# Square sums behind the FFN's first product copies, residuals from PSUM, and samples' states one by one, in a hybrid decoder layer

## The chip, the core and the metric

The kernel runs on one core of a Trainium2 chip. A core has TensorE (PE), which multiplies matrices into PSUM; VectorE (DVE), ScalarE (ACT) and GpSimd (POOL), which work on elements; and SyncE (SP), from which this kernel issues its DMAs. Each engine takes its own instructions strictly in the order in which the program lists them, and waits on semaphores for the others. The metric is the device time of one execution in microseconds, the median of some runs.

## The reference

One layer of a hybrid decoder, for a prompt of 16 + 1024 rows and 8 samples of 8 rows, each row 1024 wide. What matters here:

```
proj = rmsnorm(h) @ w_in                  # short convolution and SSD inputs
ya   = group_rmsnorm(gate_b * conv(gate_c * hv))
y, s = ssd_chunked(...)                   # chunks of 128; a state per head, sample and prompt
yb   = group_rmsnorm((y + D * xs) * silu(z))
mix  = concat(ya, yb) @ w_out
h    = h + rmsnorm(mix, norm_mix_post)
fn   = rmsnorm(h, norm_ffn_pre)
f    = (silu(fn @ w_gate) * (fn @ w_up)) @ w_down
h    = h + rmsnorm(f, norm_ffn_post)
```

Each rmsnorm multiplies a row by the inverse root of its mean square and by a weight. The outputs are the new rows and the new states.

## The kernel before

The kernel is written with pools of named tiles. A planner, which runs when the program is built, puts the instructions of each engine in order by priorities and by its own estimate of their times, places the tiles, and adds the semaphores. `high_priority(offset=n)` moves the instructions of a block ahead by n places in that order. So the order on the chip is fixed, but not the one in which the code is written, and an edit in one place can move instructions elsewhere. Products in float32 accuracy are made of three matmuls each, on a rounded high part and a low rest of both factors; each such split is a copy on ACT and a subtraction on DVE.

There are 10 tiles of rows: 0 is the 16 meta rows, 1 to 8 are the prompt, 9 is the samples. The work goes through these stages.

- *Projection and chunks.* The product with `w_in` (line 220) fills PE throughout. In between lie the SSD chunks 1 to 8 (`ssd_chunk`, with high priority HP1), and behind each chunk some of the 8 pieces of the samples' states (`sample_state(u)`, priority HP2). The table SAMP says which piece follows which chunk: one behind chunks 1, 2, 5 and 6, two behind 3 and 4. A piece loads states (tile s0, line 747), transposes them on PE into the PSUM tile s0p (line 750), splits them (s0t, lines 752 to 755), adds the update from PE's tile s1p (lines 760 to 766), stores them through SP (line 769), and multiplies by the samples' C (line 773). Two pieces in a row share the masked tiles bm1 and bm2, which the even one builds (line 740). s0p and s1p come from a pool of two PSUM tiles of two banks each, which the chunks use too. The chunk loads its decay matrix M with a DMA (line 548); DVE and ACT work on it at lines 553 to 558.

- *Output projection.* GROUPS are three groups of three tiles, (1, 2, 3), (4, 9, 5) and (6, 7, 8). For each group the 12 blocks of `w_out` are loaded and split (lines 995 to 1000) and multiplied with the three tiles' mix (line 1009), each tile into two accumulators of 512 columns. `bank` gives out accumulators in turn: positions 0 and 1 of each six are single banks, the other four are halves of two-bank tiles. Each group starts at position 2, so its first and second tile get one two-bank tile each, and the third gets two single banks. In the last group's last block the order of tiles is 8, 6, 7. After a group, `h_tile` copies each tile's two halves from PSUM into the SBUF tile h, one half on ACT (line 887), one on DVE (line 888).

- *Residual and second norm.* `residual(i, h)` takes the square sum of h on ACT (line 147, instructions named ms), the root on POOL (line 141, mr), scales h on DVE (line 899), adds the input rows (line 900) and stores h through SP (line 901). `fn_tile(i, h)` takes a second square sum (hs), root (hr), and scales into hn (line 916). PE transposes hn into the PSUM tile fT (line 928), from which ACT copies the plain transposed rows xr (line 933) and splits follow (lines 936 and 937). All square sums write their squares into one junk tile. For the first two groups this runs inside the next group's matmuls; for the last group it stands where the FFN begins, with priority HP4.

- *FFN.* The products with `w_gate` and `w_up` are made from seven products of half matrices (a Strassen-like scheme) in 11 steps. For the first three steps one of the seven, and its extension, is made ahead by `first(q)`: for x = g and u, PE multiplies the first half into the accumulator (called xg or xu, line 1050), ACT copies it out as p1g or p1u (line 1079); then PE adds the second half onto the same accumulator, ACT takes Silu of one (line 1083) and DVE the product (line 1084). The operands of `first` come from tiles 1 to 4 and 9, so the first one doesn't need the last group. It stands in the code between the last group's residuals and its `fn_tile`s. Then DVE forms sums of the xr's (T1 to T4, B22, lines 1194 to 1204 and 1190 to 1191) and of the weights (line 1091 and on; their splits, named s2g and so on, at lines 1042 and 1043), and `rest(q)` makes the other products (yg, yu, zg, zu). In two places the first column of a tile is written from p1u ahead of the tile itself (line 1189): that holds the tile's instructions behind p1u.

- *Down projection* (line 1393) and the last norm.

Of the kernel before, what the change touches and what calls it, by code (L numbers as in the profile page):

```python
# [8 lines left out]
F32 = mybir.dt.float32  # L9
# [7 lines left out]
P = 128  # L17
# [19 lines left out]
NACC = 2  # L37
YB = 1
SKIP = NMETA - 4
SAMP = {1: (0,), 2: (1,), 3: (2, 3), 4: (4, 5), 5: (6,), 6: (7,)}  # L40
LATE = (9,)
WIDE = True
SORD = "c0 c1 v0 v1 b0 c2 b1 v2 c3 v3 b2 b3"
# [13 lines left out]
def hymba_kernel(ctx, tc, x_prompt, x_sample, state_sconv, state_ssm_conv, state_ssm, meta_tokens,  # L57
# [79 lines left out]
    def rstd_of(ss, w, d, name):  # L137
        v = tp.tile([P, 1], F32, tag="rv", name=name, bufs=4)
        V.tensor_scalar(out=v[:w], in0=ss[:w], scalar1=1.0 / d, scalar2=EPS, op0=ALU.mult, op1=ALU.add)
        r = tp.tile([P, 1], F32, tag="rr", name=name + "r", bufs=4)  # L140
        G.tensor_tensor(out=r[:w], in0=v[:w], in1=mhalf[:w], op=ALU.pow)
        return r

    def square_sum(pool, src, w, name):
        junk = pool.tile([P, DM], BF16, tag="junk", name=name + "j", bufs=1)
        ss = tp.tile([P, 1], F32, tag="ss", name=name, bufs=6)
        S.activation(junk[:w, :], src, AF.Square, accum_out=ss[:w])
        return ss
# [49 lines left out]
    def bank(name):  # L198
        q = turn[0] % 6
        turn[0] += 1  # L200
        if q < 2:
            return ps.tile([P, 512], F32, tag="acc", name=name, bufs=NACC)
        if q % 2 == 0:
            turn[1] = big(name)
        return turn[1][:, (q % 2) * 512:(q % 2) * 512 + 512]
# [676 lines left out]
    def h_tile(i, pts):  # L882

        t0, w = TT[i]
        h = ph.tile([P, DM], F32, tag="h", name=f"h{i}", bufs=3)
        if w == P:
            S.activation(h[:, 0:512], pts[0], AF.Copy)
            V.tensor_copy(h[:, 512:], pts[1])
        else:
            for c in range(2):  # L890
                merge(h[:w, c * 512:(c + 1) * 512], pts[c], w, f"hm{i}{c}", ph)
        return h

    def residual(i, h):
        t0, w = TT[i]
        r = rstd_of(square_sum(ph, h[:w, :], w, f"ms{i}"), w, DM, f"mr{i}")
        xt = ph.tile([P, DM], F32, tag="tok", name=f"xt2{i}", bufs=3)
        SY.dma_start(xt[:w, :], x_rows(i))
        V.scalar_tensor_tensor(out=h[:w], in0=h[:w], scalar=r[:w], in1=post_bc[:w], op0=ALU.mult, op1=ALU.mult)
        V.tensor_tensor(out=h[:w], in0=h[:w], in1=xt[:w], op=ALU.add)  # L900
        SY.dma_start(d_h[i][:, :], h[:w])

# [6 lines left out]

    psf = []  # L910

    def fn_tile(i, h):
        t0, w = TT[i]
        xt = ph.tile([P, DM], F32, tag="tok", name=f"hn{i}", bufs=3)
        r = rstd_of(square_sum(ph, h[:w, :], w, f"hs{i}"), w, DM, f"hr{i}")
        V.scalar_tensor_tensor(out=xt[:w], in0=h[:w], scalar=r[:w], in1=ffn_bc[:w], op0=ALU.mult, op1=ALU.mult)
        late = i in GROUPS[-1]
        if late:
            both = psf[0].tile([P, 2, 512], F32, tag="pr", name=f"fT{i}", bufs=4)
        for q in range(2):  # L920
            if late:
                pt = both[:, q, :]
            else:
                pt = ps.tile([P, 512], F32, tag="small", name=f"fT{i}{q}", bufs=NSM)[:, :]
            pt = pt.rearrange("p (k t) -> p k t", k=4)
            for k in range(4):
                kk = 4 * q + k
                PE.transpose(pt[:, k, :w], xt[:w, kk * P:(kk + 1) * P], ident[:w, :w])
            for n, cs, ts in pieces(i):
                if q == 1 and i == GROUPS[-1][1]:  # L930
                    V.tensor_copy(xr[q][n][:, :, cs], pt[:, :, ts])
                else:
                    S.activation(xr[q][n][:, :, cs], pt[:, :, ts], AF.Copy)
                if n == 0:
                    bh, bl = (b[:, :, cs] for b in B1[q])
                    S.activation(bh, pt[:, :, ts], AF.Copy)
                    V.tensor_tensor(out=bl, in0=pt[:, :, ts], in1=bh.bitcast(F32), op=ALU.subtract)
# [49 lines left out]
    load_mix("b", GROUPS[0])  # L987
    for gi, tiles in enumerate(GROUPS):
        turn[0] = 2
        accs = {i: [bank(f"o{i}{c}") for c in range(2)] for i in tiles}  # L990
        for n, k in enumerate([4, 5, 6, 7, 8, 9, 10, 11, 0, 1, 2, 3]):
            nv = vec[:, 72 + k:73 + k]
            with tc.high_priority(offset=HPW):
                raw = wp.tile([P, DM], F32, tag="raw", name=f"wo{k}", bufs=3)
                SY.dma_start(raw, w_out[k * P:(k + 1) * P, :])
                hi = wp.tile([P, DM], F32R, tag="whi", name=f"woh{k}", bufs=2)
                lo = wp.tile([P, DM], F32R, tag="wlo", name=f"wol{k}", bufs=2)
                S.activation(hi, raw, AF.Copy, scale=nv)  # L998
                V.scalar_tensor_tensor(out=lo, in0=raw, scalar=nv, in1=hi[:, :].bitcast(F32), op0=ALU.mult,  # L999
                                       op1=ALU.subtract)  # L1000
            if n == 11 and gi + 1 == len(GROUPS):
                tiles = tiles[2:] + tiles[:2]
            for i in tiles:
                mh, ml = mix["b" if k >= 4 else "a", i]
                kb = k - 4 if k >= 4 else k
                steps = [(mh, hi), (mh, lo)] + ([(ml, hi)] if ml is not None else [])
                for q, (l, r_) in enumerate(steps):
                    for c in range(2):
                        PE.matmul(accs[i][c], l[:, kb, :], r_[:, c * 512:(c + 1) * 512],  # L1009
                                  start=n == 0 and q == 0, stop=n == 11 and q == len(steps) - 1)  # L1010
            if n == 1:
                load_mix("a", tiles)
            if n in (2, 6) and gi == 0:
                for q in LATE if n == 2 else FIN[9]:
                    finish(q)
            if n == 9 and gi + 1 == len(GROUPS):
                for x in "gu":
                    early_weights(x, 0)
            if n == 5 and gi + 1 < len(GROUPS):
                load_mix("b", GROUPS[gi + 1])  # L1020
            if n in RES and len(pend) > RES.index(n):
                residual(*pend[RES.index(n)])
            if n in FNS and len(pend) > FNS.index(n):
                fn_tile(*pend[FNS.index(n)])
        if gi + 1 == len(GROUPS):
            with tc.high_priority(offset=HPW):
                for x in "gu":
                    early_weights(x, 1)
        pend = [(i, h_tile(i, accs[i])) for i in tiles]

# [131 lines left out]
            residual(*args)  # L1164
    first(0)
    with tc.high_priority(offset=HP4):
        for args in pend:
            fn_tile(*args)
    first(1)
    phx.__exit__(None, None, None)  # L1170
    pmx.__exit__(None, None, None)
# [288 lines left out]
```

## Time and profile before

| | us |
|---|---|
| median of 3 runs | 1406.01 (1403.69 to 1406.12) |
| profiled execution | 1402.11 |
| its span, first to last instruction | 1400.4 |
| PE busy | 1369.7 |
| DVE busy | 973.9 |
| ACT busy | 586.2 |

A row of the timeline gives start and duration in us, engine, source line, operation, the tile written and the tiles read (out<-in), the shape and the number of instructions merged; in brackets the idle time of the engine just before it and the instruction that ended it. A row of the waits gives engine, line and tile that waited, the instruction that it waited for, the total in us, the number of waits and the longest. A row of the windows gives a stretch, its length, the busy time of PE, of PE's weight loads, of DVE, ACT and POOL with the number of their instructions, then TensorE's granted clock as a share of full speed, the DMA engines' share and GB/s. A row of one source line gives engine, operation and count, the shortest, median and longest duration in ns, and the first and last start. A busy PE is not PE at its peak, since its matmuls are pipelined and their ends are modelled.

### The profile page before, as it was taken

Reading aid. Unit: us, or ns where it says so; the run is one execution under the profiler, and the core shown is the slowest. Engines: PE = TensorE matmul, PEld = TensorE weight load, DVE = VectorE, ACT = ScalarE, POOL = GpSimd, SP = SyncE. Lnnn points to the kernel's source line nnn. Section 1 sums busy time; section 2 is a strip of 40 time slices with the busy share of each in tenths; the row PEclk is TensorE's granted clock in tenths of the full one; section 3 lists DMA queues with packets and bytes.
Section 4 is the critical chain, followed back from the end, with each engine's and each line's share of the span. In section 5 each row is a group of like instructions: output and inputs, shape, how many; then the busy total and the mean of one; then the engine's idle time right before and its main releaser. Section 6 shows DMA issues by size and latency. Waiting matters only on the chain.

```text
span 1400.4 us, 22011 instructions
## 1 busy us (share of the span) xinstructions
PE 1369.7 (98%) x8841; PEld 1230.6 (88%) x8841; DVE 973.9 (70%) x1334; ACT 586.2 (42%) x947; POOL 51.8 (4%) x106
## 2 busy tenths in 40 slices
PE   7999999999999999999899999999999999999997
PEld 5889998878888988887799999999999998888886
DVE  6654457868888988767689877666767666455565
ACT  6465345434354354656553232222332334344431
POOL 1000000000000200011100000000000000000001
PEclk9999999999999999999999999999999999999999
DMA  6135346667746457765435553444433479655554
GB/s 214 47 109 148 95 125 198 202 178 205 218 117 208 123 185 256 237 226 196 154 119 167 203 207 113 149 167 168 145 136 103 159 226 341 208 180 165 170 165 139
DMA packets 212543, 240.51 MB, mean 172 GB/s; under 512 B 33421, under 2 KB 161505, under 8 KB 212442
## 3 DMA queue, kind: packets, MB, share of 16 engines
q1 hardware_dynamic: 212442, 239.12, 53.5%
q8 instruction: 69, 1.13, 0.3%
q14 instruction: 32, 0.26, 0.1%
HBM read 170.29 MB, written 68.79 MB: 171 GB/s over the span
## 4 chain that ended last, share of the span: by engine, by line
PE 90%; DVE 3%; DMA 3%; ACT 2%; issue 1%; SPq 1%; POOL 0%; DVEq 0%; POOLq 0%; ACTq 0%
PE d L1393 15%; PE px L220 10%; PE o L1009 9%; PE yu L1050 7%; PE yg L1050 7%; PE pz L220 5%; PE zu L1050 5%; PE zg L1050 5%; PE xg L1050 5%; PE xu L1050 5%; PE pb L220 3%; PE pc L220 3%; PE ph L220 2%; DMA M<-d_a 1%; PE pd L572 1%
## 5 line engine op out<-in xcount | busy, mean ns | idle before, releaser
L220 PE MATMUL px<-xh,whi 128*128 128x272 f32 (+2 forms) x288 | 94.6, 336 | 0.1
L220 PE MATMUL px<-xl,whi 128*128 128x272 f32 (+2 forms) x288 | 93.7, 333 | 0.0
L220 PE MATMUL px<-xh,wlo 128*128 128x272 f32 (+2 forms) x288 | 93.3, 332 | 0.0
L98 DVE TENSOR_TENSOR wlo<-raw,whi 128x1024 fp32r<-128x1024 f32 x32 | 39.0, 1220 | 45.5 <-ACT whi L106 45.4
L999 DVE SCALAR_TENSOR_TENSOR wol<-wo,vec,woh 128x1024 fp32r<-128x1024 f32 x36 | 46.0, 1278 | 32.2 <-ACT woh L998 32.1
L220 PE MATMUL pz<-xh,whi 128*128 128x256 f32 (+2 forms) x192 | 64.6, 337 | 0.0
L220 PE MATMUL pz<-xh,wlo 128*128 128x256 f32 (+2 forms) x192 | 63.9, 333 | 0.0
L220 PE MATMUL pz<-xl,whi 128*128 128x256 f32 (+2 forms) x192 | 63.7, 332 | 0.0
L998 ACT ACTIVATE woh<-wo,vec 128x1024 fp32r<-128x1024 f32 x36 | 41.4, 1149 | 49.1 <-PE o L1009 45.9
L220 PEld LDWEIGHTS px<-xh,whi 128*128 128x128 f32 x288 | 54.4, 192 | 4.6 <-ACT xr L279 0.3
L220 PEld LDWEIGHTS px<-xl,whi 128*128 128x128 f32 x288 | 53.9, 190 | 4.2 <-issue 0.2
L220 PEld LDWEIGHTS px<-xh,wlo 128*128 128x128 f32 x288 | 54.0, 190 | 3.7
L1393 PE MATMUL d<-wd,B01h 128*128 128x512 f32 x176 | 54.2, 389 | 0.0
L252 DVE SCALAR_TENSOR_TENSOR xa<-xr,vec,xa 128x1128 f32<-128x1128 f32 x36 | 50.1, 1391 | 1.2 <-ACT xa L249 0.5
L1393 PE MATMUL d<-wd,T3h 128*128 128x512 f32 x152 | 46.8, 389 | 0.0
L1009 PE MATMUL o<-wol,mhb 128*128 128x512 f32 x144 | 44.4, 394 | 0.2 <-DVE wol L999 0.2
L1393 PE MATMUL d<-wd,B11h 128*128 128x512 f32 x144 | 44.1, 389 | 0.0
L1393 PE MATMUL d<-wd,T2h 128*128 128x512 f32 x144 | 44.1, 389 | 0.0
L279 ACT ACTIVATE xr<-px 128x272 f32<-128x272 f32 (+2 forms) x36 | 16.3, 456 | 60.4 <-PE px L220 60.3
L556 ACT ACTIVATE M<-M,a_tok 128x128 f32<-128x128 f32 (+1 forms) x72 | 21.7, 382 | 46.0 <-DMA M<-d_a 45.1
L1009 PE MATMUL o<-woh,mlb 128*128 128x512 f32 x128 | 40.3, 392 | 0.0
L220 PEld LDWEIGHTS pz<-xh,whi 128*128 128x128 f32 x192 | 36.1, 188 | 3.9 <-issue 1.3
(691 smaller groups left out, 4101.3 us busy)
## 6 DMA issues: line engine op xcount, KB each, us to landing
wo<-in_w_out_dram SPq DMA_DIRECT2D x36, 512.0 KB, 4.8
raw<-in_w_in_dram SPq DMA_DIRECT2D x32, 512.0 KB, 5.3
wg<-in_w_gate_dram SPq DMA_DIRECT2D x11, 1024.0 KB, 8.5
wu<-in_w_up_dram SPq DMA_DIRECT2D x11, 1024.0 KB, 5.3
xr<-in_w_down_dram SPq DMA_DIRECT2D x11, 1024.0 KB, 5.6
d_t<-xr SPq DMA_DIRECT2D x11, 1024.0 KB
xt<-in_x_prompt_dram SPq DMA_DIRECT2D x16, 512.0 KB, 4.8
M<-d_a SPq DMA_DIRECT2D x16, 512.0 KB, 5.4
```

Of the source, the lines that this page charges most:

```text
L98: V.tensor_tensor(out=out, in0=a, in1=hi.bitcast(F32), op=ALU.subtract)
L220: PE.matmul(acc, (hi, lo, hi)[q][:, wk], (xh, xh, xl)[q][t][:, k, o:], start=n_ == 0, stop=n_ + 1 == len(order))
L252: V.scalar_tensor_tensor(out=dst, in0=part(row, i), scalar=wv[:, wcol(i):wcol(i) + 1], in1=dst, op0=ALU.mult, op1=ALU.add)
L279: S.activation(row[:, rc], pt[:, pc], AF.Copy)
L556: S.activation(M[:w, h, :w], M[:w, h, :w], AF.Relu, scale=-1.0, bias=a_s)
L572: PE.matmul(pdv[64 * e:64 * e + 64, h // 2, :w], xd[:w, h * 64:(h + 1) * 64], Ms[h // 8][:w, h % 8, :w], start=True, stop=True)
L998: S.activation(hi, raw, AF.Copy, scale=nv)
L999: V.scalar_tensor_tensor(out=lo, in0=raw, scalar=nv, in1=hi[:, :].bitcast(F32), op0=ALU.mult, op1=ALU.subtract)
L1009: PE.matmul(accs[i][c], l[:, kb, :], r_[:, c * 512:(c + 1) * 512], start=n == 0 and q == 0, stop=n == 11 and q == len(steps) - 1)
L1050: PE.matmul(acc[:, c, 0:W1], w_[l][k], b[r_][:, k, c * W1:(c + 1) * W1], start=start and k == 0 and x == 0, stop=k == 3 and x == 2, skip_g ...
L1393: PE.matmul(accs[t], sx[x][:, tl], wx[y], start=st and x + y == 0, stop=en and x == 1, skip_group_check=n not in OPENS)
```

## The change

Three edits. First, `square_sum` can be given a tile `behind`: it then writes the first column of its junk tile from that tile before it squares. For the last group, in the order 8, 6, 7, the second square sums are given p1g, p1u and p1u of `first(0)`. Second, those tiles of the last group whose two accumulators are one two-bank tile (6 and 7) are no longer copied by `h_tile`; their `residual` takes the square sum and the scaling straight from PSUM and writes h from there. Tile 8 is copied as before. Third, in SAMP the pieces 3 and 4 follow chunk 4, and 5, 6 and 7 follow chunks 5, 6 and 7; chunk 3 has piece 2 alone.

```diff
-SAMP = {1: (0,), 2: (1,), 3: (2, 3), 4: (4, 5), 5: (6,), 6: (7,)}
+SAMP = {1: (0,), 2: (1,), 3: (2,), 4: (3, 4), 5: (5,), 6: (6,), 7: (7,)}
...
-    def square_sum(pool, src, w, name):
+    def square_sum(pool, src, w, name, behind=None):
         junk = pool.tile([P, DM], BF16, tag="junk", name=name + "j", bufs=1)
+        if behind is not None:
+            S.activation(junk[:, 0:1], behind[:, 0, 0:1], AF.Copy)
         ss = tp.tile([P, 1], F32, tag="ss", name=name, bufs=6)
         S.activation(junk[:w, :], src, AF.Square, accum_out=ss[:w])
...
-    def residual(i, h):
+    def residual(i, h, src=None):
         t0, w = TT[i]
-        r = rstd_of(square_sum(ph, h[:w, :], w, f"ms{i}"), w, DM, f"mr{i}")
+        src = h if src is None else src
+        r = rstd_of(square_sum(ph, src[:w, :], w, f"ms{i}"), w, DM, f"mr{i}")
...
-        V.scalar_tensor_tensor(out=h[:w], in0=h[:w], scalar=r[:w], in1=post_bc[:w], op0=ALU.mult, op1=ALU.mult)
+        V.scalar_tensor_tensor(out=h[:w], in0=src[:w], scalar=r[:w], in1=post_bc[:w], op0=ALU.mult, op1=ALU.mult)
...
-    def fn_tile(i, h):
+    def fn_tile(i, h, behind=None):
...
-        r = rstd_of(square_sum(ph, h[:w, :], w, f"hs{i}"), w, DM, f"hr{i}")
+        r = rstd_of(square_sum(ph, h[:w, :], w, f"hs{i}", behind), w, DM, f"hr{i}")
...
-        accs = {i: [bank(f"o{i}{c}") for c in range(2)] for i in tiles}
+        accs, pairs = {}, {}
+        for i in tiles:
+            accs[i] = [bank(f"o{i}{c}") for c in range(2)]
+            if turn[0] % 6 != 2:
+                pairs[i] = turn[1]
...
-        pend = [(i, h_tile(i, accs[i])) for i in tiles]
+        if gi + 1 < len(GROUPS):
+            pend = [(i, h_tile(i, accs[i])) for i in tiles]
+        else:
+            pend = [(i, h_tile(i, accs[i])) if i not in pairs else
+                    (i, ph.tile([P, DM], F32, tag="h", name=f"h{i}", bufs=3), pairs[i]) for i in tiles]
...
-        for args in pend:
-            fn_tile(*args)
+        for args, x in zip(pend, "guu"):
+            fn_tile(*args[:2], p1s[x, 0])
```

## The prediction

> **What bounds the kernel now.** I read the page first, then TensorE's waits, then the windows around each wait, and last the order of instructions on ScalarE (ACT), VectorE (DVE) and TensorE (PE) there.
>
> ```profile
> span 1400.4 us, 22011 instructions
> PE 1369.7 (98%) x8841; PEld 1230.6 (88%) x8841; DVE 973.9 (70%) x1334; ACT 586.2 (42%) x947; POOL 51.8 (4%) x106
> ...
> PE xg L1050 <- ACT p1g L1079: 5.7, 1, 5.7
> ...
> PE s0p L750 <- DVE s L766: 2.9, 1, 2.9
> PE yg L1050 <- DVE s2g L1043: 2.6, 1, 2.6
> ...
> PE so L773 <- ACT s0t L752: 1.4, 1, 1.4
> ```
>
> PE is busy for 1369.7 of 1400.4 us, so 30.7 us is all that any reordering could win. The change adds and removes no matmul. It can only touch PE's waits, and the two largest single ones are the ones it aims at: 5.7 us where the FFN begins and 2.9 us among the samples' states. The profiled execution took 1402.1 us (span 1400.4 and 1.7 around it); the median of the runs is 1406.0, 3.9 above it. I work in differences and add them to the median.
>
> **The start of the FFN, as it is.**
>
> ```profile
> 685.43 0.61 PE L1009 MATMUL o<-woh,mla 128*128 128x512 f32 x2
> ...
> 688.89 0.41 PE L1050 MATMUL xu<-B01h,weuh 128*128 128x272 f32 x2
> 697.75 0.82 PE L1050 MATMUL xg<-B11h,wegh 128*128 128x272 f32 x2 [5.69 <-ACT p1g L1079]
> ...
> 700.41 0.73 PE L928 MATMUL fT<-ident,hn 128*128 128x128 f32 x4
> 705.74 1.03 PE L928 MATMUL fT<-ident,hn 128*128 128x128 f32 x8
> ...
> 685.05 1.06 ACT L147 ACTIVATE ms8j<-h 128x1024 bf16<-128x1024 f32 x1 [0.41 <-DVE h L888]
> 688.01 1.06 ACT L147 ACTIVATE ms6j<-h 128x1024 bf16<-128x1024 f32 x1
> 696.04 1.06 ACT L147 ACTIVATE hs6j<-h 128x1024 bf16<-128x1024 f32 x1 [3.27 <-DVE h L900]
> 697.09 0.60 ACT L1079 ACTIVATE p1g<-xg 128x544 f32<-128x544 f32 x1
> ```
>
> The first half of xg was done at 688.9, when xu began. Its second half adds onto the same PSUM and must wait until ACT has copied the first out (p1g). That copy stood in ACT's queue behind hs6, the second square sum of tile 6, and hs6 waited until 696.04 for DVE. PE stood from 692.06 to 697.75. The wait has a second price, in the granted clock:
>
> ```profile
> 302.30:306.00 3.70, 3.69 (x27) 3.59 (x28) 3.70 (x5) 2.78 (x4) 0.00 (x0) 1.00 0.80 239
> 697.70:700.20 2.50, 2.45 (x11) 2.45 (x11) 1.93 (x4) 1.55 (x3) 1.10 (x2) 0.50 0.98 313
> 700.20:703.00 2.80, 2.80 (x24) 2.80 (x23) 1.35 (x2) 1.81 (x2) 0.00 (x0) 0.92 0.49 147
> 735.10:738.60 3.50, 3.46 (x16) 3.46 (x17) 3.50 (x6) 0.00 (x0) 0.00 (x0) 0.56 0.63 242
> ```
>
> The number after the busy times is the clock. Behind the 5.69 us wait it was 0.50 for 2.5 us and 0.92 for 2.8: 1.25 + 0.22 = 1.47 us lost. Behind the 2.61 us wait (yg) 0.56 for 3.5 us: 1.54 lost. Behind the 2.87 us wait (s0p, ended 302.3) it stayed 1.00.
>
> **Part 1: the hold.** Tile 8's second square sum now stands behind p1g on ACT, tiles 6's and 7's behind p1u, since their junk tile is first written from these copies. ACT is free for p1g once ms7 is done, at 689.4 if the three ms sums follow one another (686.2 + 3 x 1.06 for ms6, weight split, ms7); the copy ends at 690.0, before PE has finished xu at 692.0. So the 5.69 us go, and 1.47 of clock with them: 7.16. Added are three copies of one column:
>
> ```profile
> 726.71 0.20 ACT L1189 ACTIVATE T1h<-p1u 128x1 fp32r<-128x1 f32 x1
> ...
> 686.00:740.00 54.00, 45.52 (x341) 44.87 (x340) 45.49 (x46) 30.50 (x45) 4.10 (x6) 0.94 0.37 126
> ```
>
> 3 x 0.20 us, which I count as nothing: ACT has 30.5 of 54 us busy here. Without that cover they would delay hs6 and hs7 by 0.6. Queued behind a held square sum on ACT are the evictions of the transposes, which need that sum anyway. On SP the three stores of h and the weight load behind them move with DVE's add, in unchanged number and order.
>
> **What is late next.** The normalized tiles hn8, hn6, hn7, which PE transposes between the FFN's matmuls.
>
> ```profile
> 686.53 0.55 POOL L141 TENSOR_TENSOR mr8r<-mr,mhalf 128x1 f32<-128x1 f32 x1 [32.36 <-DVE mr L139]
> ...
> 686.72 0.69 DVE L888 COPY h<-o 128x512 f32<-128x512 f32 x1 [0.33 <-ACT h L887]
> 687.33 1.28 DVE L899 SCALAR_TENSOR_TENSOR h<-h,mr8r,post_bc 128x1024 f32<-128x1024 f32 x1
> 689.66 0.69 DVE L888 COPY h<-o 128x512 f32<-128x512 f32 x1
> 690.26 1.22 DVE L900 TENSOR_TENSOR h<-h,xt 128x1024 f32<-128x1024 f32 x1
> 692.27 1.28 DVE L899 SCALAR_TENSOR_TENSOR h<-h,mr6r,post_bc 128x1024 f32<-128x1024 f32 x1 [0.49 <-POOL mr6r L141]
> 697.00 1.28 DVE L916 SCALAR_TENSOR_TENSOR hn<-h,hr8r,ffn_bc 128x1024 f32<-128x1024 f32 x1
> 700.27 1.28 DVE L916 SCALAR_TENSOR_TENSOR hn<-h,hr7r,ffn_bc 128x1024 f32<-128x1024 f32 x1
> 707.01 2.42 DVE L1194 TENSOR_TENSOR xr<-xr,xr 128x2176 f32<-128x2176 f32 x1 [5.46 <-ACT xr L933]
> ```
>
> From 687.33 to 701.55 DVE is the chain: three scalings, three additions, a weight split, three hn, at 1.2 us a step. hn8 is ready at 698.28. In the kernel before PE came to its first transposes at 700.41, because it had been held up. Without that wait it comes there earlier than hn8 does.
>
> **Part 2: residuals from PSUM.** Tiles 6 and 7 (whose two accumulators lie in one two-bank tile; tile 8's don't) lose their copies: two on ACT and two on DVE. On DVE the one at 686.72 frees 0.25 (tile 8's scale came from POOL at 687.08), that at 689.66 frees 0.60 (689.66 to 690.26), and ms6 no longer waits for a copy, so the 0.49 before 692.27 goes: 1.3 us, and hn8 is ready at 697.0, hn7 at 700.2. Square sum and scaling with a PSUM source are not in this trace; the nearest row is a subtraction with a PSUM source of that size, against the same with both in SBUF (690.26, 1.22):
>
> ```profile
> L753 DVE TENSOR_TENSOR s0p<-s0p,s0t x8: 1221/1226/1233, 245.2 to 454.3; 128x1024 f32<-128x1024 f32 x8
> ```
>
> 1.226 against 1.22: I take the difference as nothing. [...] The two PSUM tiles are held until the scaling of their tile ends, near 689.7 and 692, instead of 687.4 and 690.3. If the planner gives one of the FFN's first accumulators that place, xu waits from 688.9 to 689.7 or even 692: 0.8 to 3.1 us. If it is given to the transposes, which need the scaled tiles anyway, nothing. I take nothing: xg, 3.0 us before xu and so at 685.9, began before any copy of tiles 6 and 7 was done, so its place was another's.
>
> **The sum at the FFN.** How far into the second half the planner puts the first transposes decides. Before, they stood after 5.5 of xg's 12 pairs (697.75 to 700.41); a pair takes 0.25 us at full clock, so there PE would arrive at 692.0 + 1.4 = 693.4 and wait 3.6 us for hn8. Put behind all 12 pairs, it arrives at 695.0 and waits 2.0. Held square sums come later in the plan too, so transposes go back rather than forward; I take the middle, 2.8 us. By the 2.61 us wait such a gap costs the clock, some 1.47; by the 2.87 us wait not. I take that it does, as these two gaps lie among the same kind of matmuls. 7.16 - 2.8 - 1.47 = 2.9 us won.
>
> [...]
>
> The wait before yg stays:
>
> ```profile
> 729.73 2.42 DVE L1191 TENSOR_TENSOR T1l<-xr,T1h 128x2176 fp32r<-128x2176 f32 x1
> 734.40 0.68 DVE L1043 TENSOR_TENSOR s2g<-sg,s2g 128x512 fp32r<-128x512 f32 x1
> 735.14 1.27 PE L1050 MATMUL yg<-T2h,s2g 128*128 128x272 f32 x4 [2.61 <-DVE s2g L1043]
> ```
>
> From 707.01, when the last xr arrives, DVE works nearly without a break to s2g at 735.08, 28.1 us. xr comes from the transposes (705.74), which come some 3 us earlier with PE; both move together: 0, bounded by 2.61 + 1.54 won or 3 lost.
>
> **Part 3: samples one by one.**
>
> ```profile
> 302.31 1.09 PE L750 MATMUL s0p<-ident,s 128*128 128x128 f32 x8 [2.87 <-DVE s L766]
> ...
> 296.93 0.29 DVE L553 TENSOR_SCALAR M<-M,a_tok 128x128 f32<-128x128 f32 x1 [4.60 <-DMA M<-d_a]
> 301.03 1.22 DVE L766 TENSOR_TENSOR s<-s1p,s 128x1024 f32<-128x1024 f32 x1
> ...
> SPq L769 <- DVE s L766: 38.6, 7, 10.7
> ```
>
> In chunk 3 the second sample's transposes wait for the PSUM tile of the first, which DVE frees late because it stood 4.60 us behind the load of M. With one sample in chunk 3 no second one waits: 2.87 us won, no clock. The store of a sample's state blocks SP up to 10.7 us, with the next weight load behind it; with one sample per chunk this is rarer, though moved past other loads. The pair is now in chunk 4 (states 3 and 4). Chunk 4 held a pair before (4 and 5), with no wait on PE. I price the new pair at 0, its bound being another 2.87. The 1.4 us wait of so on s0t lay in chunk 5, which still has one state: 0, bounds -1.4 and +1.4.
>
> **The forecast.** 2.9 + 2.9 = 5.8 us won: 1402.1 becomes 1396.3, the median 1406.0 becomes 1400.2.
>
> **Rivals.** (a) *All is won*: the transposes are planned past hn8's arrival, so no wait takes the place of p1g's. 7.16 + 2.87 = 10.0: 1396.0. For it: hs6 and hs7 are planned later. Against: hn7 must still be waited for.
>
> (b) *Nothing is left*: the transposes keep their place (3.6 + 1.47 of the 7.16 are given back, 2.1 remain) and the pair in chunk 4 repeats the 2.87 less a little. 1406.0 - 2.1 = 1403.9 with ordinary shifts of a microsecond or so from a new plan on either side: within 0.2% or just outside. That the hold doesn't bring p1g forward at all gives the same time.
>
> (c) *Slower: DVE overflows at the end of the chunks.* State 5 moves to chunk 5, 6 to 6, 7 to 7.
>
> ```profile
> 441.00:500.00 59.00, 59.00 (x403) 50.69 (x402) 50.91 (x64) 26.82 (x56) 7.57 (x3) 1.00 0.51 159
> 500.00:542.00 42.00, 42.00 (x247) 35.28 (x246) 40.27 (x47) 22.81 (x30) 2.39 (x2) 1.00 0.56 195
> ```
>
> A state costs DVE four steps of 1.2 us (301.03 is one) and some small ones, about 5.8. DVE has 1.7 us free between 500 and 542. If state 7 falls there, DVE is 4.1 late, and with one stall like the 4.60 for M 8.7; PE's output projection then waits for its weight and mix splits, with 1.5 of clock: 10.2 lost against 5.8 won, 1410.4. It decides from 8.6 us of lateness and clock on (then 1408.8). Against it: DVE has 8.1 us free between 441 and 500, where the states can go.
>
> (d) *The clock stays up* behind the new wait, as it did behind the 2.87 us at 302.3: 1400.2 - 1.47 = 1398.7. For it speaks that gap, against it the 2.61 us one.
>
> **How the numbers follow.** This measurement can tell about 0.2%, 2.8 us, from no change: 1403.2 to 1408.8. Chances: forecast 0.30, (a) 0.18, (b) 0.25, (c) 0.15, (d) 0.12. Faster: 0.30 less 0.03 for a forecast that falls short, 0.18, 0.12 and 0.08 of (b), 0.65. Same: 0.17 of (b), the 0.03, and 0.02 of (c), 0.22. Slower 0.13. The range runs from (a) with 2 us of the yg wait won too, 1394.0, to 1407.0, which holds (b) with the bound of xu's wait (3.1). Left out is (c). The forecast's own range is 1397 to 1403.
>
> **What would show it.** Right: p1g directly after ms7 on ACT; no 5.7 us wait of xg on p1g; a wait of about 2 to 4 us at fT on DVE's hn8 instead, the clock low behind it; hn8 near 697; no L888 copies for tiles 6 and 7; no wait of s0p near 302; yg's wait about as long. Wrong: fT waits for nothing (a), PE's s0p of state 4 waits for L766 (b), waits of o on wol or the mix tiles before 560 (c), or xu waiting at 688.9 for a PSUM tile.

## The result, and the profile after

The changed kernel takes 1416.05 us (median of 6 runs, 1414.17 to 1420.02), the kernel before 1406.07 (1403.69 to 1409.21). The ratio is 1.0074, with an interval of 1.0055 to 1.0093: about 10 us slower, where 5.8 us faster was forecast, and outside the range. The profiled execution took 1417.24 us.

The head of the page, and the lines of PE's waits that answer to those shown of before (in all, times, the longest):

```profile
span 1415.5 us, 22006 instructions
PE 1378.6 (97%) x8841; PEld 1235.8 (87%) x8841; DVE 974.0 (69%) x1332; ACT 585.2 (41%) x948; POOL 53.4 (4%) x106
...
PE px L507 <- DVE s L768: 4.1, 1, 4.1
...
PE pz L222 <- DVE z L629: 2.9, 1, 2.9
PE o L1016 <- ACT mhb L957: 2.8, 1, 2.8
...
PE fT L931 <- DVE hr L139: 2.1, 1, 2.1
...
PE o L1016 <- DVE mlb L98: 1.1, 1, 1.1
...
PE xg L1061 <- ACT p1g L1090: 0.7, 1, 0.7
...
PE yg L1061 <- DVE s2g L1054: 0.2, 1, 0.2
```

The two waits that the change aimed at are gone or small, 5.7 us at xg and 2.9 at s0p, and so is the 2.6 at yg, which was to stay. Ahead of the FFN stand four waits that were not there, 4.1, 2.9, 2.8 and 1.1 us; in the FFN, the 2.1 at fT that was forecast is new. PE's busy time is 8.9 us longer with the same 8841 instructions, about half of it the clock (0.992 on average against 0.995, some 4 us of the span). The windows by stage (busy time of PE, PEld, DVE, ACT, POOL; then the clock, the DMA share and GB/s), first before, then after:

```profile
300.00:400.00 100.00, 96.27 (x713) 82.82 (x714) 79.37 (x112) 46.09 (x81) 1.55 (x4) 1.00 0.66 180
540.00:560.00 20.00, 20.00 (x91) 16.12 (x90) 15.83 (x20) 7.34 (x9) 0.00 (x0) 1.00 0.84 283
560.00:580.00 20.00, 20.00 (x90) 16.57 (x89) 13.13 (x14) 9.86 (x11) 0.00 (x0) 1.00 0.84 269
```

```profile
300.00:400.00 100.00, 91.14 (x626) 78.25 (x625) 75.10 (x110) 45.38 (x85) 2.08 (x4) 0.97 0.57 165
460.00:500.00 40.00, 38.53 (x274) 33.19 (x272) 36.64 (x43) 15.28 (x27) 8.20 (x3) 1.00 0.51 151
540.00:560.00 20.00, 15.97 (x66) 11.43 (x65) 19.46 (x22) 9.16 (x12) 0.00 (x0) 0.97 0.84 311
560.00:580.00 20.00, 20.00 (x79) 16.28 (x78) 13.26 (x16) 7.90 (x9) 0.00 (x0) 0.86 0.94 274
```

Two stretches lost most: chunks 3 and 4 (300 to 400 us: 5.1 us of PE and 3% of the clock) and the first matmuls of the output projection (540 to 580: 4.0 us of PE, 3% of the clock, then 14%). Another 1.5 us of PE went between 460 and 500. From 540 to 560 DVE was busy for 19.46 of 20 us. The FFN's first xg comes at 705.51 where it came at 685.88; it begins 19.6 us later (1.6 of that from the start of the program), and the program ends 15.1 us later. So the FFN gave back 4.5 us, and the part before it lost 18.

**Chunks 3 and 4.** DVE, then PE, in the kernel after:

```profile
300.28 0.29 DVE L555 TENSOR_SCALAR M<-M,a_tok 128x128 f32<-128x128 f32 x1 [5.80 <-DMA M<-d_a]
301.62 1.46 DVE L555 TENSOR_SCALAR M<-M,a_tok 128x128 f32<-128x128 f32 x7
302.99 1.29 DVE L766 TENSOR_TENSOR s<-s,ES 128x512 f32<-128x512 f32 x2
304.38 1.23 DVE L768 TENSOR_TENSOR s<-s1p,s 128x1024 f32<-128x1024 f32 x1
...
330.45 1.66 DVE L555 TENSOR_SCALAR M<-M,a_tok 128x128 f32<-128x128 f32 x8 [2.23 <-DMA M<-d_a]
...
332.63 2.09 DVE L742 TENSOR_TENSOR bm<-bt,bd 64x512 fp32r<-64x512 f32 x3
334.75 1.23 DVE L755 TENSOR_TENSOR s0p<-s0p,s0t 128x1024 f32<-128x1024 f32 x1
335.89 0.41 DVE L629 SCALAR_TENSOR_TENSOR z<-z,pz 128x256 f32<-128x256 f32 x1
```

```profile
305.66 1.66 PE L507 MATMUL px<-ident,xb 128*128 128x128 f32 x8 [4.07 <-DVE s L768]
...
336.36 0.50 PE L222 MATMUL pz<-xh,whi 128*128 128x512 f32 x1 [2.94 <-DVE z L629]
```

The update of state 2 (L768) frees a two-bank PSUM tile, and it stands on DVE behind the load of M, as before. Only the one that waits for this tile is another: without a second state in chunk 3 the next taker in PE's order is px, the first step of chunk 4. It waits 4.07 us where s0p waited 2.87. Thirty microseconds later PE waits for z, which stands on DVE behind another wait for M (2.23 us), the masks bm that state 4 builds, and a split of state 3 (L755).

The second of these waits is the new one. Taken over all runs below that leave M's first step on DVE, the wait for L768 is there with either table: 2.07 to 4.53 us at s0p where states 2 and 3 both follow chunk 3, 2.20 to 4.07 at px where state 3 follows chunk 4. But z waits 2.67 to 3.33 us in each of the six runs with state 3 behind chunk 4 (the change, e2, e5, e8, e10, e13), and never more than 1.1 us in the others.

**The output projection.** DVE's groups by line from 538 to 558 us, the reciprocals of the short convolution's norm first before, then after:

```profile
L672 DVE RECIPROCAL sq<-sq 128x160 f32<-128x160 f32 (+1 forms) x4 | 5.5, 1413 | 0.0
```

```profile
L674 DVE RECIPROCAL sq<-sq 128x128 f32<-128x128 f32 (+3 forms) x7 | 10.6, 1548 | 1.0 <-ACT sq L671 1.0
L98 DVE TENSOR_TENSOR mlb<-mrb,mhb 128x1024 fp32r<-128x1024 f32 x2 | 2.4, 1220 | 0.5 <-ACT mhb L957 0.5
```

Chunk 8's state product was issued at 522.09 us, 17 later than before (504.99), and the mix tiles' pool opens in the code only where the pool of the chunks closes, behind chunk 8: their first loads were issued at 539.20, before at 517.64. Before, DVE split the first two at 525.69, while the projections pb of the short convolution still kept PE busy (25 matmuls of each of their three kinds lie between 520 and 540 us). After, it came to them at 546.35, and to the next two at 558.12, behind the reciprocals of those same projections. By then pb was nearly used up (8 of each kind between 540 and 560), and PE had nothing else to do. The longer of PE's two waits there, 2.77 us, ended with ACT's copy mhb of the third tile, which had itself waited for the load; the 1.12 us behind it is DVE's split.

```profile
555.91 1.06 ACT L957 ACTIVATE mhb<-mrb 128x1024 fp32r<-128x1024 f32 x1 [1.26 <-DMA mrb<-d_yb]
```

### The profile page after: what moved, and what is told of

The parts are those of the page before. It is cut to its first block, busy times and chain, and to the rows that moved or that the text cites. A ratio compares the mean times of both kernels' runs of the same rounds, so it can differ in the third digit from the quotient of the medians.

```text
span 1415.5 us, 22006 instructions
## 1 busy us (share of the span) xinstructions
PE 1378.6 (97%) x8841; PEld 1235.8 (87%) x8841; DVE 974.0 (69%) x1332; ACT 585.2 (41%) x948; POOL 53.4 (4%) x106
## 4 chain that ended last, share of the span: by engine, by line
PE 84%; DVE 7%; DMA 4%; ACT 3%; issue 2%; SPq 0%; POOL 0%; DVEq 0%; POOLq 0%; ACTq 0%
PE d L1404 14%; PE px L222 10%; PE o L1016 9%; PE yg L1061 7%; PE yu L1061 7%; PE pz L222 5%; PE zg L1061 4%; PE zu L1061 4%; PE xg L1061 4%; PE xu L1061 4%; PE pc L222 3%; DMA M<-d_a 2%; PE pb L222 2%; PE ph L222 1%; PE pd L574 1%
## 5 line engine op out<-in xcount | busy, mean ns | idle before, releaser
L1016 PE MATMUL o<-woh,mhb 128*128 128x512 f32 x144 | 41.3, 410 | 3.1 <-ACT mhb L957 2.8
```

## The experiments

Ratios are to the kernel before on the same chip; differences between kernels are the difference of the ratios times 1406 us.

**The halves.** The FFN edits with the old table (e1_old_samp), the new table alone (e2_new_samp), the hold alone (e3_hold), the PSUM residuals alone (e4_psum).

```
e1: the changed kernel with
+SAMP = {1: (0,), 2: (1,), 3: (2, 3), 4: (4, 5), 5: (6,), 6: (7,)}
e2: the kernel before with
+SAMP = {1: (0,), 2: (1,), 3: (2,), 4: (3, 4), 5: (5,), 6: (6,), 7: (7,)}
e3: the kernel before, in square_sum and fn_tile
...
+            S.activation(junk[:, 0:1], behind[:, 0, 0:1], AF.Copy)
...
e4: the kernel before, in residual (tiles 6 and 7: src is the PSUM pair)
+        V.scalar_tensor_tensor(out=h[:w], in0=src[:w], scalar=r[:w], ...)
...
```

> The changed kernel with the old table of samples' states: held square sums and residuals from PSUM alone. Theory (the two halves of the change are independent, the states cost it): the FFN's gain alone, as in the changed trace's drift between output projection and end, 4.5 us: about 1401.5, ratio 0.9968. Rival (the loss comes with the re-planned FFN or the PSUM tiles held longer): 1406 or more. No wait of 4 us on L768, none of 2.8 us on mhb by the theory.

> The kernel before with the new table of samples' states alone. Theory: the whole loss, undiminished: the output projection reached 16 to 19 us later, 1421 to 1425. Rival (the loss needs both halves): under 1416. The FFN's waits as before: 5.7 us on p1g and 2.6 on s2g by the theory.

> The kernel before with the held square sums alone. Theory: the hold removes the 5.7 us wait of xg on p1g, but hn8 is ready 1.3 us later than with PSUM reads, so PE waits some 3.4 us at fT instead of 2.1: about 1403, 3 us faster than before. Rival (the hold is the whole gain): 1401.5.

> The kernel before with the residuals read from PSUM alone. Theory: p1g still stands behind hs6 on ACT, which waits for DVE, now 1.3 us less: the wait of xg is 4.4 instead of 5.7 us: about 1404.7. Rival (the earlier sums re-order ACT so that p1g comes first anyway): 1401.5.

| kernel | us | ratio (interval) |
|---|---|---|
| e1, FFN edits | 1398.33 | 0.9957 (0.9941 to 0.9973) |
| e2, table | 1421.33 | 1.0110 (1.0090 to 1.0130) |
| e3, hold | 1402.44 | 0.9979 (0.9966 to 0.9993) |
| e4, PSUM residuals | 1404.71 | 0.9997 (0.9986 to 1.0009) |

The FFN edits win 6 us, the table loses 15.5 (16.4 by the difference of e1 and the change), and the two add up to the whole within a microsecond. Nothing of the loss comes from the FFN. By the medians the FFN edits are worth more together (6.0) than apart (3.0 and 0.4), but the intervals (3.8 to 8.3, 1.0 to 4.8, -1.3 to 2.0) don't separate the sum. Alone, the PSUM residuals led the planner to put the first transposes ahead of xg's second half, and one wait took the place of another (it stands in the first half of xu):

```profile
702.69 1.08 PE L931 MATMUL fT<-ident,hn 128*128 128x128 f32 x4 [7.14 <-DVE hr L139]
```

**Which sample.** Five tables, all with the FFN edits, to be set against e1 with the old table:

```
e5:  {1: (0,), 2: (1,), 3: (2,), 4: (3, 4), 5: (5,), 6: (6, 7)}
e6:  {1: (0,), 2: (1,), 3: (2, 3), 4: (4, 5), 5: (6,), 7: (7,)}
e8:  {1: (0,), 2: (1,), 3: (2,), 4: (3, 4, 5), 5: (6,), 6: (7,)}
e9:  {1: (0,), 2: (1,), 3: (2, 3), 4: (4, 5), 6: (6, 7)}
e12: {1: (0,), 2: (1, 2), 3: (3,), 4: (4, 5), 5: (6,), 6: (7,)}
```

> The changed kernel with piece 7 behind chunk 6 again, beside piece 6 (3 and 4 behind chunk 4, 5 behind 5 as changed). Theory: the loss of 16.4 us from the table has two places, chunk 4's start (wait of 4.1 on L768, 2.9 on z, clock: some 7) and the output projection's start (2.8 + 1.1 on the mix splits, clock: some 8), and piece 7 behind chunk 7 makes the second. So 1398.3 + 7 to 9: 1406, with no wait on mhb. Rival (piece 7's place does nothing): 1414 to 1416.

> The changed kernel with the old table but for piece 7, behind chunk 7 instead of 6. Theory: the loss at the output projection's start alone, some 8 us: 1406, with waits on mhb and without the waits at chunk 4. Rival (it was the pair's shift to chunk 4 that made chunk 8 late): 1398 to 1400.

> The changed kernel with the old table but for piece 3, behind chunk 4 with 4 and 5. Theory: chunk 4's px takes the PSUM tile that piece 3 used to wait for, so the wait on L768 stays, on px instead of s0p, and is longer, with a wait on z behind it: some 7 us over the old table, 1405. Rival (the loss is the end's alone): 1398 to 1400.

> The changed kernel with the old table but for piece 6, behind chunk 6 with piece 7, none behind chunk 5. Theory (two pieces behind chunks 6 and 7 make chunk 8 late, and the output projection's first mix tiles with it, since the pool that holds them opens only behind chunk 8): chunk 8's state product comes at 514 or later instead of 507, waits on mhb or mlb return, 1404 to 1407 against 1399 with the old table. Rival (the end's loss follows from the lost time at chunk 4, which this table doesn't have): 1398 to 1400.

> The changed kernel with one piece more ahead of chunk 4 rather than behind it: 1 and 2 behind chunk 2, 3 behind chunk 3, the rest as of old. Theory: chunk 8 is on time, so nothing is lost at the end; piece 2 or chunk 4's px may wait for the update before it, one wait of 2 to 4 us as in the old table: 1397 to 1402. Rival (any other table than the old one re-plans the fill and loses): 1404 or more.

| kernel | us | ratio (interval) | over e1 | PE busy 300 to 400, clock | PE busy 540 to 560 |
|---|---|---|---|---|---|
| old table (e1) | 1398.33 | 0.9957 | | 95.77, 0.98 | 20.00 |
| one by one (the change) | 1416.05 | 1.0074 | 16.4 | 91.14, 0.97 | 15.97 |
| e5 | 1417.35 | 1.0075 (1.0058 to 1.0091) | 16.6 | 91.59, 0.98 | 12.83 |
| e6 | 1403.38 | 0.9974 (0.9962 to 0.9985) | 2.4 | 94.48, 1.00 | 19.47 |
| e8 | 1411.45 | 1.0033 (1.0015 to 1.0052) | 10.7 | 92.38, 0.97 | 19.16 |
| e9 | 1412.00 | 1.0056 (1.0035 to 1.0076) | 13.9 | 93.08, 0.97 | 14.48 |
| e12 | 1408.09 | 1.0016 (1.0004 to 1.0029) | 8.3 | 97.53, 1.00 | 15.16 |

The two columns on PE come from one profiled execution each, and not each is typical: that of e9 took 1417.67 us, 5.7 above its median, and that of e16 further below 1406.11, 5.3 under its median.

My theory after the first runs was that state 7 in chunk 7 makes the end late. It fell: e5 has it in chunk 6 again and is no faster, and e6 has it in chunk 7 and loses only 2.4 us. That the loss needs state 2 alone in chunk 3 fell with e9. e8, e9 and e12 each came out above what I had expected of them. What the table shows instead is that the two stretches lose separately. e12 loses nothing in chunks 3 and 4 (97.53 busy, full clock) and 8.3 us in all, by waits at the output projection; e8 loses 10.7 with hardly a wait there. All the other tables lose something, e6 no more than the noise allows (the intervals overlap); I found no rule by which the number of states in a chunk gives the time.

**The M step moved to ACT** (e7_M_on_act): the changed kernel with both halves of M's first step on ACT, the same arithmetic, so that L768 no longer stands behind it.

```
...
-                if g == 0:
-                    V.tensor_scalar(out=M[:w, h, :w], in0=M[:w, h, :w], scalar1=a_s, ...
+                S.activation(M[:w, h, :w], M[:w, h, :w], AF.Relu, scale=-1.0, bias=a_s)
...
```

> The changed kernel with the decay matrix's first step on ACT for both halves, so that DVE doesn't stand behind the load of M. Theory: piece 2's update then runs in time, the wait of chunk 4's px on L768 (4.1) and its clock loss go, and with 72 fewer DVE steps (15 us) the end of the chunks is relieved too: 1406 to 1411. Rival (DVE waits for M at the next step anyway): px waits as before, 1414 to 1418.

Measured 1414.16 us, 1.0059 (1.0039 to 1.0078). The wait of px was gone and PE busy for 95.68 us of the stretch from 300 to 400 at a clock of 1.00, yet the time fell by 2 us only, which is within the noise. The second place kept its loss and added to it: PE was busy for 16.69 us at a clock of 0.83 from 540 to 560, and for 18.05 from 560 to 580 (in the change 15.97 at 0.97, and 20.00 at 0.86).

**DVE lightened** (e10_no_recip with the new table, e11_old_no_recip with the old): the reciprocals of the short convolution's norm become copies. Both kernels thus leave that norm out.

```
-                V.reciprocal(sq[:, h], sq[:, h])
+                V.tensor_copy(sq[:, h], sq[:, h])
```

> The changed kernel with the short convolution's reciprocals left out (a copy in their place, so its norm is wrong): 15 DVE steps of 0.9 to 3.3 us between 424 and 546 become short, about 20 us of DVE. If DVE's load makes chunk 8 late, the waits on the mix tiles and their clock loss go: 1408 to 1411. If chunk 8 is late because the pieces hold the two PSUM tiles that it needs, it stays late and the waits stay: 1414 to 1416. The loss at chunk 4 stays in both.

> The control to it: the same copy in place of the reciprocals, with the old table. Nothing in the old table's stretch from 424 to 690 waits for DVE by more than 1 us, so both theories expect the old table's time, 1398 to 1400. The difference between the two tables is then read without the reciprocals: some 10 us if DVE's load made the end's loss, 16 if not.

New table 1407.85 us, 1.0019 (1.0006 to 1.0031); old table 1399.51, 0.9959 (0.9946 to 0.9973), no different from e1. So the reciprocals cost the old table nothing, and the new one half its loss: the table costs 8.4 us without them, 16.4 with them. The windows of the two, first e10, then e11:

```profile
300.00:400.00 100.00, 92.21 (x643) 79.21 (x644) 74.07 (x104) 43.47 (x78) 2.29 (x4) 0.97 0.58 170
540.00:560.00 20.00, 20.00 (x90) 16.02 (x90) 11.40 (x20) 9.86 (x12) 0.00 (x0) 1.00 0.86 315
```

```profile
300.00:400.00 100.00, 95.29 (x687) 81.46 (x686) 77.71 (x114) 47.07 (x85) 0.86 (x4) 1.00 0.64 177
540.00:560.00 20.00, 20.00 (x91) 16.14 (x90) 11.46 (x16) 7.72 (x10) 0.00 (x0) 1.00 0.76 249
```

From 540 to 560 us DVE now has 11.4 us of work and PE doesn't wait for the mix tiles, although chunk 8 is still late (515.59 for its state product, against 522.09 in the change and 504.99 before). It takes both, then: late mix tiles, and reciprocals ahead of their splits. e12, with the reciprocals, loses there though its first split comes little later than in e10 (539.70 against 537.37). e6 has the reciprocals (10.6 us of them between 540 and 560) but its first o at 533.79, and hardly waits. What is left in e10 is the stretch from 300 to 400. This is the counterpart of e12: one run has only the first loss (8.4), one only the second (8.3), and their sum is 16.7 against 16.4 for both. That it fits so closely is in part luck: e12 is another table, with waits of its own, each of the two figures is uncertain by more than 2 us, and e8 loses 10.7 with hardly a wait in the second stretch.

**The mix tiles loaded in place** (e13_in_place, e14_earlier_in_place, e15_old_in_place). The mix tiles pass through two raw tiles, so that each pair of loads waits for the splits of the pair before. Here they are loaded into the tile of their low part, of which there are four: into the change, the table of e12, and e1 as a control.

```
...
-            raw = pm.tile([P, nb, P], F32, tag="mr" + part, name=f"mr{part}{i}", bufs=2)
+            if w == P and part == "b":
+                ml = pm.tile([P, nb, P], F32R, tag="ml" + part, name=f"ml{part}{i}", bufs=4)
+                lo, raw = ml, ml[:, :, :].bitcast(F32)
...
```

> The changed kernel with one thing taken away: the mix tiles of the output projection are loaded straight into the tile of their low part (four of them) instead of into two raw tiles, so a load no longer waits until an earlier tile's two splits are through; the same arithmetic. In the changed kernel the mix loads go two and two (539.2 and 547.7 us), o waits 2.8 us for mhb and 1.1 for mlb at 557 to 559 us, and the granted clock is 0.50 and 0.84 in the windows from 559 to 569, which costs some 3 us more. Theory (half of the table's loss is this chain of two raw tiles, met when chunk 8 comes late): the wait at 557 goes and the time falls by 5 to 8 us, to 1408 to 1411. Rival (the chain only reports that chunk 8's rows come late, and PE would wait for the first load instead): 1413 to 1418, with the wait for mhb moved to the first o matmul.

> The kernel with the samples at chunks 1, 2, 2, 3, 4, 4, 5, 6, its mix tiles loaded in place as in the run above. That table had no wait in chunk 4; its whole loss against the old table lay in the output projection: o waited 5.9 us for mhb and 0.8 for mlb between 534 and 551 us, and the clock then fell to 0.68 and 0.63 (3.0 us). Theory: most of that goes, 1399 to 1402. Rival: 1406 to 1410.

> Control: the FFN edits with the old table, its mix tiles loaded in place. There o never waits for a mix tile, since the projections of chunk 8 still to do cover the second pair of loads. Theory: no change, 1397 to 1400. Rival (the in-place load is worth something everywhere): 1392 to 1396.

1414.30 us (1.0065, 1.0044 to 1.0086), 1407.45 (1.0007, 0.9995 to 1.0020) and 1400.31 (0.9960, 0.9948 to 0.9972). The theory fell: not 5 to 8 us come back but about 1 in each of the two, which is no more than noise, and the control is unchanged. In e14 the four loads went out together, and PE then waited for the weight split on DVE:

```profile
540.47 0.74 PE L1020 MATMUL o<-woh,mhb 128*128 128x512 f32 x2 [2.51 <-ACT mhb L961]
555.45 0.73 PE L1020 MATMUL o<-wol,mhb 128*128 128x512 f32 x2 [3.06 <-DVE wol L1010]
```

```profile
550.14 3.35 DVE L674 RECIPROCAL sq<-sq 128x256 f32<-128x256 f32 x2
553.41 0.88 DVE L600 RECIPROCAL sg<-sg 128x128 f32<-128x128 f32 x1
554.22 2.37 DVE L1010 SCALAR_TENSOR_TENSOR wol<-wo,vec,woh 128x1024 fp32r<-128x1024 f32 x2
```

The split of the weights stands on DVE behind 4.2 us of reciprocals, just as the split of the mix tile did in the change. With the raw tiles out of the way DVE's queue sets this stretch.

**Both taken away** (e16_M_act_in_place: e7 and e13 together; e17_M_act_no_recip: e7 and e10 together; e18_old_M_act_no_recip: the same with the old table). Their diffs are those above.

> Both suspects of the changed kernel taken away together: both halves of the M step on ACT, so that the piece's update no longer waits on DVE behind it, and the mix tiles loaded in place. Theory (the two places carry the table's loss between them): 1399 to 1406. Rival (each place only takes over what the other lets go): 1410 to 1416.

> The changed kernel with DVE lightened at both places: both halves of the M step on ACT, and the short convolution's reciprocals replaced by copies (this leaves its norm out). Without the reciprocals alone, 8.3 us of the table's 16.4 were left, and the windows put them at 300 to 400 us (PE 92.2 busy against 95.3 with the old table, clock 0.97 against 1.00). Theory (what is left is DVE's queue in chunks 3 and 4, where the M step stands ahead of the piece's update and of z): within 4 us of the run with the old table below. Rival (the new table keeps PE waiting for DVE whatever the M step does): 6 to 9 us above it.

> The partner of the run above: the same two edits with the old table of samples. Theory and rival alike: near the old table without reciprocals, 1396 to 1401; it is there to be taken from the run above.

e16 took 1411.43 us (1.0038, 1.0024 to 1.0051): the first stretch is whole again (96.15 busy, clock 1.00), the second is not (15.62), and the time lies where the rival had it. This profile shows the fastest of the 12 executions, so its mean clock of 0.999 is not typical (0.997 over all 12). e17 took 1406.44 (1.0008, 0.9995 to 1.0022) and e18 1405.54 (0.9998, 0.9986 to 1.0009): with DVE lightened at both places the new table costs 1.4 us more than the old. That is what the theory said, but the partner wasn't where either account had it: with the old table the M step on ACT costs 5.5 us (e18 against e11), with waits for z of 5.0 us. So the two runs show that the tables come out alike when DVE is light; that the M step alone makes the first stretch's loss they don't show, since moving it costs something of its own.

## Why the prediction was wrong, step by step

**Part 3 failed.** It counted the wait of s0p as won: "With one sample in chunk 3 no second one waits". The wait belonged to the PSUM tile that L768 frees, not to the second state. The tile's next taker became px, which waited 4.07 us, and this time the clock fell with it (0.55 from 305.66 to 309.30). I asked what is late next for the FFN, and not here. Nor is 2.87 a fixed size, or "no clock" a safe reading: s0p's wait was 2.07 to 4.53 us in the eight kernels with states 2 and 3 behind chunk 3; in e1 it was 3.4 us, and the clock from 300 to 400 us was 0.98 there, against 1.00 before. "I price the new pair at 0, its bound being another 2.87" failed too: the pair's step in chunk 4 stood ahead of z, which waited 2.94 us and which the prediction doesn't name. Most missing of all from its sum is the output projection: a later chunk 8 was looked at in rival (c) alone. In place of 2.9 us won, the runs show 16.4 lost, about half in chunks 3 and 4 and half at the output projection.

**Rival (c) was the nearest**, with the place right (waits of o on the mix splits at 557 to 559, before 560), the engine right (DVE), and a total of 1410.4. But it held state 7 in chunk 7 to be the cause, which e5 and e6 refute, and spoke against itself with "DVE has 8.1 us free between 441 and 500". That mean is still there in the change (36.64 of 40 busy from 460 to 500). It says nothing of the 20 us that decide, in which DVE was full. Nor does a full DVE decide by itself: before, it was busy for 20.00 of 20 us from 520 to 540, and PE lost nothing there, since it still had pb to do. The chance of 0.15 was too small, and the range left it out. Rival (b) was right that the pair brings a wait, but it came at z and not at state 4's s0p, and its price was too low.

**Part 1 held.** p1g follows ms7 on ACT (708.82 in the change), the wait of 5.69 us is gone, and the new one at fT is 2.08 us, where 2.8 was forecast (2.0 for transposes behind all 12 pairs; they stand a little later still, in xu). Its clock was charged, and in the change (0.71 from 717.77 to 720.80, 0.74 to 724.00) and in e1 it did fall; here in e1, where the FFN is the same and nothing before it disturbs:

```profile
700.98:704.00 3.02, 3.02 (x14) 3.02 (x15) 1.65 (x3) 1.72 (x3) 1.10 (x2) 0.52 0.00 0
704.00:707.00 3.00, 3.00 (x26) 3.00 (x25) 1.71 (x2) 1.36 (x3) 0.00 (x0) 0.92 0.05 18
```

That is 1.45 + 0.24 = 1.69 us, against 1.47 forecast; rival (d), by which the clock stays up, did not hold in these two. But that the charge came out right was partly luck. The same wait of 2.08 us left the clock up in e15, and one of 2.1 us in e16, where the clock averages 0.999 over the profiled execution; here are the 8 us behind it, first in e1, then in e15:

```profile
700.98:708.98 8.00, 8.00 (x55) 8.00 (x55) 5.09 (x5) 3.30 (x6) 1.10 (x2) 0.79 0.18 55
703.95:711.95 8.00, 7.35 (x58) 6.99 (x59) 5.70 (x5) 3.71 (x7) 1.09 (x2) 1.00 0.23 68
```

The reason given in the prediction, that the gaps lie among the same kind of matmuls, therefore doesn't decide it.

**Part 2 held.** The scaling from PSUM takes as long as from SBUF (in the change 1.285 and 1.278 us against 1.285), the square sum rather less (1.000 and 1.024 us against 1.06); the scalings in e1:

```profile
689.96 1.28 DVE L902 SCALAR_TENSOR_TENSOR h<-h,mr8r,post_bc 128x1024 f32<-128x1024 f32 x1 [0.73 <-POOL mr8r L141]
...
694.02 1.28 DVE L902 SCALAR_TENSOR_TENSOR h<-o,mr6r,post_bc 128x1024 f32<-128x1024 f32 x1 [0.38 <-POOL mr6r L141]
```

xu waited for no PSUM tile. hn8 came 12.1 us after the first xg (700.84 against 688.72 in e1), where 11.1 was worked out (697.0 against 685.9): 0.72 of the difference is DVE's wait for POOL's root hr8r just ahead of hn8, which the prediction left out.

**The yg wait did not stay.** The forecast priced it at 0 with a bound of 2.61 + 1.54 = 4.15 won; in the change it is 0.15 us, and the clock behind it stays at 1.00 (735 to 760 us). In its place are two waits, in e1 of 0.71 (xg) and 1.44 us (yg, on u3g), which kept the clock (1.00 from 723.59 to 731.00 behind the first, from 752.88 to 757.00 behind the second). So the FFN's sum is 7.16 - 2.08 - 1.69 + 4.0 - 0.71 - 1.44 = 5.2 us. The traces show 4.4 (from the first xg to the end 714.5 us before, 710.1 in e1), the runs 6.0 (3.8 to 8.3); the forecast was 2.9. The mechanism was right, the term of yg mis-sized. It was put at 0 because PE and DVE would move together; what moved was DVE's order. Before, T1l and B22l (2.42 us each, at 729.73 and 732.07) stood ahead of s2g; in the change s2g stands ahead of them:

```profile
746.10 0.69 DVE L1054 TENSOR_TENSOR s2g<-sg,s2g 128x512 fp32r<-128x512 f32 x1
...
750.91 2.42 DVE L1202 TENSOR_TENSOR T1l<-xr,T1h 128x2176 fp32r<-128x2176 f32 x1
```

Why the planner chose so was not tried. Nor is all of the 6.0 us the FFN's waits: over their executions the granted clock averages 0.997 in e1 and 0.994 before, which is some 4 us of it.

**What stays open:** why so small a move of a state (e9 differs from e6 only in states 6 and 7) makes some 11 us (by the ratios). The planner's order changes with each table, and I can say where the loss is met, not what a table must look like. That M's load makes the first stretch's loss was not separated from the planner's other moves there; loading M earlier, into one more tile, wasn't tried.

## What to carry to other kernels

A wait for a buffer belongs to the buffer's release: taking the waiting work away can hand the wait to the next taker in the engine's order, as here from s0p (2.87 us) to px (4.07), so name that one and price it before counting the gain. A mean over sixty microseconds hides a queue: whether an engine off the critical path can take work in is read from windows as short as the cover of the one that waits for it, and together with that cover. Keep what the halves show: the FFN edits with the old table of samples (1398.33 us, 0.9957) beat both kernels.

## What the runs showed of the hardware

How long a gap of PE costs the clock has no sharp bound here. The clock fell behind the waits of 5.69 us (before, to 0.50), 4.07 and 2.94 us (the change, 0.55 in the windows below), 3.06 us (e14, 0.59 from 555.45 to 559.00) and 2.61 us (before, 0.56), and not behind those of 2.87 us (before, 1.00) and 2.80 us (e16, 1.00 from 540 to 560); the wait of 2.08 us at fT did both, as shown above. Short of the kernel's end, each fall in the traces of before and of the change is to 0.50 and lasts 3.41 us, but for one of 6.83 (the change, behind the waits of 2.77 and 1.12 us at o), and within each of the two the falls begin whole multiples of 3.41 us apart (before, 186 and 197 steps behind the first; in the change 71, 80, 145 and 192). The first fall of each had no wait of 1 us ahead of it from 30 us on: it came at 62.3 us before and at 63.6 in the change, 1.4 and 1.1 us behind 2.17 us of matmuls of 16 columns each (0.57 from 62.84 to 66.25 before, 0.56 from 63.30 to 66.70 in the change). No run here moved a gap by itself, so what decides whether a wait of 2 to 3 us costs the clock was not shown. After the waits at px (4.07 us) and pz (2.94) in the change:

```profile
305.66:309.30 3.64, 3.64 (x17) 3.64 (x18) 3.64 (x4) 2.71 (x4) 0.00 (x0) 0.55 0.78 236
336.36:340.00 3.64, 3.64 (x9) 2.89 (x10) 2.70 (x3) 1.63 (x4) 0.00 (x0) 0.55 0.43 126
```

So a new wait of 2 to 3 us is priced with and without its 1.7 us of clock (half of 3.41), and the clock of one profile is not taken for that of all executions: the 12 of e17 run from 1401.66 us at a mean clock of 0.999 to 1411.21 at 0.994. A reciprocal on DVE is dear as well: 3.35 us for two of 128x256 elements (e14), where a scaling of 128x1024 from two tensors and a column took 1.28 (the change).
